# A hybrid decoder block in one pass: fp32r transposes, padded 64-row products, other first loads and separate loads in the output

## The chip, the cores and the metric

The kernel runs on one core of a Trainium2 chip. Its time is the device time of one execution in microseconds; where several executions are given, the median counts. The core has five engines that work side by side and wait for each other by semaphores: TensorE (PE) multiplies matrices out of SBUF into PSUM, VectorE (DVE), ScalarE (ACT) and GpSimd (POOL) work on rows, and SyncE (SP) issues the DMA transfers between device memory and SBUF.

## The reference

One block of a decoder, for one sequence of 1024 tokens with 1024 channels. The input is normalised and projected to 4104 columns. One half of the result feeds eight heads of stick-breaking attention, the other half four heads of a gated delta rule. Both results are normalised per head, gated, put side by side, projected back, added to the input and normalised.

```python
h = rmsnorm(x, norm1_w[layer])
proj = jnp.einsum('btd,de->bte', h, w_in[layer])
sb_q, sb_k, sb_v, sb_z, g_q, g_k, g_v, g_z, g_b, g_a = jnp.split(proj, split_idx, axis=-1)
...
o_sb = rmsnorm(o_sb.transpose(0, 2, 1, 3), sb_norm_w[layer]).reshape(b, t_len, SB_WIDTH)
o_sb = o_sb * jax.nn.silu(sb_z)
...
o_gdn = gated_delta_chunked(gq, gk, gv, decay, beta)
o_gdn = o_gdn * jax.nn.silu(g_z)
mixed = jnp.concatenate([o_sb, o_gdn], axis=-1)
x = x + jnp.einsum('bte,ed->btd', mixed, w_out[layer])
return rmsnorm(x, final_norm_w)
```

The attention weight of key s for query t is `sigmoid(z_ts)` times the product of `1 - sigmoid(z_tj)` over the keys between them. The delta rule works in chunks; for each chunk a unit lower triangular matrix is inverted, and a state of 128 by 128 per head runs from chunk to chunk.

## The kernel before

**Numbers.** Large products are made of three fp32r products: each operand is split into a high part (rounded to fp32r) and a low part (the rest), and high x high, high x low and low x high are summed in PSUM (`mm3`). The splitting is done by ACT (the rounding copy) and DVE or POOL (the subtraction). Small products are made in f32, which takes two passes each on TensorE.

**First stage.** x comes transposed in eight blocks of 128 channels (`xr`, from `xT`), beside the blocks of the query weights (`wq`) and the gain (`n1`). `LOADS` is the order in which the loads are issued, and `later` lets an operation in a queue only behind another one. Block 0 comes in two halves. Each block is scaled and split into `xh` and `xl`, and the eight query products grow in eight banks of PSUM. Meanwhile x comes a second time in rows, for the sums of squares. Then eight weight blocks `wcr` (columns of beta, decay and value) are split into the two halves of `chl`: the high part by ACT, the low part by DVE (blocks 0 and 1) or POOL (blocks 2 to 7), 520 columns at a time; the first 264 are used for the first value product, the others later, in `values`. When the norm is known, the raw blocks are scaled on DVE by gain and norm and split again into `xh` and `xl`.

**Fill.** The other projections are made in column groups of 128, in the order of the list `ORDER` (G: the delta heads' k, q and v; v: the second half of the values; k: attention keys; z: gates). They fill TensorE whenever no other stream has something ready.

**Delta rule.** For each head and half of the sequence, `gdn_pre` has q and k in a tile `kq` (four places in the pool `gd`), turns them on TensorE as f32 against the identity, and takes the sums of squares. `gdn_sub` and `gdn_inv` make the inverse of eight chunks: 16-row blocks by substitution on POOL, then 32, then 64, then 128 rows. The last step is two products per chunk over 64 rows: `y2p` from the lower left block of the matrix and the upper inverse (`W`, rows 0 to 63 of `wy`), and `x2p` from that and the lower inverse. The inverse stands in the tile `xinv` (`X`). `gdn_chain` then runs the state through the chunks.

**Attention.** For each head four windows of two query blocks; the scores are turned into weights by two sigmoids (ACT), a scan (DVE) and a product (POOL), then turned on TensorE as fp32r words (`turned`, with `Fixed.words`, which gives a second tile of type fp32r in the same place) and multiplied with the values.

**Output.** `out_weights` loads and splits the eight blocks of the output weights, first 4 to 7 (delta), then, once the projections are over, 0 to 3 (attention), in one stream. For each of the eight token blocks `enter_delta` loads the delta result (`mx`), the gate (`gt`) and the input row block (`xr`); `split` turns the four quarters of `mx` as f32 (`turned`), multiplies with the gate, and splits. `products_delta` adds 24 products per block to `xr`. `enter_attention`, `prepare(0)` and `products_attention` do the same for the attention half; the last adds the squares, multiplies by the inverse root and the final gain, and stores. `mx` and `gt` have three places in the pool `f0` and three in `f1`. The last block is cut in three pieces (512, 320 and 192 columns).

**Order.** The program writes the order of every engine by a planner of its own: the streams at the end of `block` are run by `interleave` against a model of the engines (`Model`, with a price for each operation in `cost`), and the order in which the model starts the operations is fixed for each engine. Streams with a smaller first number go first on TensorE; the second number is the priority of what they issue on the other engines. All DMA is issued on SP. So a change of a price or of a stream deals out the whole order anew. The profile puts almost every instruction on line 355, where the planner's recorder issues it; so the tiles' names tell them apart.

Of the kernel before, what the change touches and what calls it, by code (L numbers as in the profile page):

```python
# [28 lines left out]
ORDER = "G0 v1 G1 k0 k1 G2 G3 k2 k3 z4 z5 z6 z7 z0 z1 z2 z3".split()  # L29
# [104 lines left out]
class Fixed:  # L134
# [10 lines left out]
    def tile(self, shape, dtype, name, tag):  # L145
# [6 lines left out]
        return self.place(shape, dtype, name, at, r)  # L152

# [317 lines left out]
def block(tc, xT_d, x_d, n1_d, wE_d, wQ_d, wC_d, conv_d, alog_d, dtb_d, mixw_d, wo_d, fnw_d, out_d):  # L471
# [4 lines left out]
    with ExitStack() as top:  # L476
# [7 lines left out]
        fx = Fixed(ck, nc, {**{f"sg{w}": (2048 * (w + 1), 1) for w in range(4)}, "o2": (1024, 1)})  # L484
# [143 lines left out]
        for k in range(NK):  # L628
# [3 lines left out]
            xr = s0.tile([P, T], F32, name=f"xr{k}")  # L632
            raw.append(xr)
            n = 1 if k else 2
            for u in range(n):
# [6 lines left out]
                V.tensor_tensor(wl[:, es], w[:, es], wh[:, es].bitcast(F32), ALU.subtract)  # L642
                A.activation(xh[:, k, hs], xr[:, hs], AF.Copy, scale=n1[:, k:k + 1])
                V.scalar_tensor_tensor(xl[:, k, hs], xr[:, hs], n1[:, k:k + 1], xh[:, k, hs].bitcast(F32), ALU.mult, ALU.subtract)
# [21 lines left out]
        ck.prio = 0.4  # L666
        for b in range(NB):
# [39 lines left out]
        for k0 in range(0, NK, 2):  # L707
# [4 lines left out]
            for k in (k0, k0 + 1):  # L712
                A.activation(xh[:, k, :], raw[k], AF.Copy)
                V.tensor_tensor(xl[:, k, :], raw[k], xh[:, k, :].bitcast(F32), ALU.subtract)
# [229 lines left out]
        def delta_load():  # L944
            yield lambda: "dec" in flags
            for h in range(GH):
                for g in range(2):
# [6 lines left out]
                    kq = gd.tile([P, 4, 2, P], F32, tag="kq", bufs=4, name="kq")  # L954
# [33 lines left out]
        def gdn_pre(h, g):  # L988
# [10 lines left out]
            nkv = gd.tile([P, 4, P], F32, tag="nkv", bufs=4, name="nkv")  # L999
            for which in range(2):  # L1000
# [86 lines left out]
        def gdn_inv(h):  # L1087
# [30 lines left out]
            G.memset(W[0:32, :, 32:64], 0.0)  # L1118
            V.tensor_copy(W[0:32, :, 0:32], wc[0:32])
# [34 lines left out]
            for c in range(8):  # L1154
                TE.matmul(yv2[64:128, c, :], nm(c, slice(0, 64), slice(64, 128)), W[:, c, :], start=True, stop=True)
# [3 lines left out]
            for c in range(8):  # L1159
                TE.matmul(xv2[0:64, c, :], wy[64:128, c, :], X[64:128, c, 64:128], start=True, stop=True)  # L1160
# [203 lines left out]
        def out_weights():  # L1364
# [5 lines left out]
            yield lambda: "proj" in flags  # L1370
# [191 lines left out]
```

## Time and profile before

| | us |
|---|---|
| median of three executions | 658.06 |
| lowest and highest | 657.96, 659.88 |
| the profiled execution | 659.28 |
| its span, first to last instruction | 657.5 |

| engine | busy us | share | instructions |
|---|---|---|---|
| PE | 645.3 | 98% | 3978 |
| DVE | 453.8 | 69% | 851 |
| ACT | 387.5 | 59% | 921 |
| POOL | 332.2 | 51% | 364 |

The profile's page gives the engines' busy time, groups of instructions and DMA queues. In a row such as `pz<-step,mx 128*128 128x128 f32 x64 | 9.6, 272 | 0.0` stand the tile written and those read, for TensorE the held matrix (rows*columns) and the moving one, the count, the busy time in us, the mean duration of one in ns, and the idle time of the engine before them. All fp32r operands of products are printed as f32. Products overlap on TensorE, so a duration is longer than the distance to the next start. An f32 product or the like is recorded as two passes, a transpose as one. In a row of the timeline stand the start, the time from the first start to the last end, the engine, the instruction and how many of a kind follow each other. The granted clock is TensorE's, 1 for full speed.

### The profile page before, as it was taken

The numbers are of one execution on the slowest core, as the hardware profiler recorded it, in microseconds if no ns is written. First come the engines' busy times: TensorE is split into PE (matmuls) and PEld (weight loads), VectorE is DVE, ScalarE is ACT, GpSimd is POOL, SyncE is SP. The second block draws the span as 40 slices with busy tenths as digits, with TensorE's granted clock in tenths as the row PEclk, the third lists the DMA queues.
The fourth block names the chain that finished last, engine by engine and source line by source line (L and its number), as shares of the span: only waits on it lengthen the run. The fifth ranks groups of instructions, "written<-read, shape, count | busy, mean of one in ns | idle before, by whom it ended". The sixth has DMA issues, their size and how long they took to land.

```text
span 657.5 us, 11705 instructions
## 1 busy us (share of the span) xinstructions
PE 645.3 (98%) x3978; PEld 553.4 (84%) x3978; DVE 453.8 (69%) x851; ACT 387.5 (59%) x921; POOL 332.2 (51%) x364
## 2 busy tenths in 40 slices
PE   8999999999999999999999999999999999999995
PEld 7889888988888887888888888989898888888785
DVE  4358984434448879888889637897878553657874
ACT  5645566844538687777696447676878541223332
POOL 0106154928776857546586748473444323127642
PEclk9999999999999999999999999999999999999999
DMA  8929337863684435433563860634243492944232
GB/s 296 336 91 364 119 124 224 303 212 112 193 276 134 151 108 160 139 107 124 182 181 79 262 198 25 211 93 147 89 138 97 147 326 92 349 144 149 96 129 96
DMA packets 97643, 111.83 MB, mean 170 GB/s; under 512 B 29552, under 2 KB 62512, under 8 KB 97584
## 3 DMA queue, kind: packets, MB, share of 16 engines
q1 hardware_dynamic: 97584, 111.09, 51.7%
q8 instruction: 31, 0.51, 0.3%
q14 instruction: 28, 0.23, 0.1%
HBM read 76.03 MB, written 35.03 MB: 169 GB/s over the span
## 4 chain that ended last, share of the span: by engine, by line
PE 87%; DVE 8%; ACT 2%; issue 2%; DMA 1%; SPq 0%; POOL 0%; POOLq 0%; ACTq 0%; DVEq 0%
PE pp L355 53%; PE pz L355 25%; PE po L355 6%; PE pc L355 3%; DVE xl L355 2%; DVE xr L355 2%; DVE cc L355 1%; DMA xr<-xT 1%; DVE pp L355 1%; ACT yj L355 0%; DVE al L355 0%; SPq L355 0%; ACT nkv L355 0%; DVE v2e L355 0%; DVE ac L355 0%
## 5 line engine op out<-in xcount | busy, mean ns | idle before, releaser
L355 PE MATMUL pp<-xh,weh 128*128 128x512 f32 x360 | 148.8, 413 | 0.1
L355 PE MATMUL pp<-xl,weh 128*128 128x512 f32 x360 | 141.3, 392 | 0.5 <-DVE xl L355 0.3
L355 PE MATMUL pp<-xh,wel 128*128 128x512 f32 x360 | 141.3, 393 | 0.0
L355 POOL TENSOR_TENSOR sgf<-sgf,cc 128x128 f32<-128x128 f32 (+3 forms) x64 | 77.3, 1210 | 72.4 <-DVE cc L355 58.8
L355 POOL TENSOR_TENSOR wel<-wer,weh 128x512 fp32r<-128x512 f32 x48 | 62.1, 1298 | 57.0 <-ACT weh L355 49.8
L355 PEld LDWEIGHTS pp<-xh,wel 128*128 128x128 f32 x360 | 67.8, 188 | 14.9
L355 PEld LDWEIGHTS pp<-xl,weh 128*128 128x128 f32 x360 | 68.0, 189 | 10.9 <-DVE xl L355 1.3
L355 PEld LDWEIGHTS pp<-xh,weh 128*128 128x128 f32 x360 | 67.8, 188 | 10.4 <-DVE ac L355 0.8
L355 ACT ACTIVATE sgf<-pz,rs 128x384 f32<-128x384 f32 (+3 forms) x96 | 53.7, 589 | 13.2 <-PE pz L355 12.5
L355 DVE TENSOR_TENSOR_SCAN cc<-pz,step 128x384 f32<-128x384 f32 (+2 forms) x64 | 53.5, 846 | 9.2 <-ACT pz L355 8.9
L355 DVE TENSOR_TENSOR al<-pz,ah 128x512 fp32r<-128x512 f32 (+1 forms) x80 | 49.8, 628 | 12.8 <-ACT ah L355 12.6
L355 ACT ACTIVATE pz<-pz,ns 128x384 f32<-128x384 f32 (+3 forms) x96 | 52.8, 567 | 0.0
L355 PE MATMUL pp<-woh,mh 128*128 128x512 f32 (+2 forms) x132 | 52.2, 395 | 0.2 <-DVE xr L355 0.2
L355 ACT ACTIVATE ah<-pz 128x512 fp32r<-128x512 f32 (+1 forms) x80 | 43.7, 559 | 12.9 <-PE pz L355 12.7
L355 PE MATMUL pp<-woh,ml 128*128 128x512 f32 (+2 forms) x132 | 50.8, 385 | 0.0
L355 PE MATMUL pp<-wol,mh 128*128 128x512 f32 (+2 forms) x132 | 50.6, 383 | 0.0
L355 DVE SCALAR_TENSOR_TENSOR pp<-pre,conv,pp 128x512 f32<-128x512 f32 x42 | 31.5, 749 | 21.3 <-ACT pp L355 20.7
L355 POOL TENSOR_TENSOR ac<-ac,pre 128x512 f32<-128x512 f32 x24 | 31.0, 1291 | 29.3 <-ACT pre L355 20.1
L355 POOL TENSOR_TENSOR ml<-mf,mh 128x512 fp32r<-128x512 f32 x16 | 21.5, 1346 | 47.0 <-ACT mh L355 46.9
L355 PE MATMUL po<-ah,v2a 128*128 128x256 f32 (+1 forms) x160 | 43.5, 295 | 0.0
L355 DVE TENSOR_TENSOR_SCAN cc<-pz,cc,step 128x512 f32<-128x512 f32 (+1 forms) x32 | 38.7, 1208 | 3.6 <-ACT pz L355 3.0
L355 PE MATMUL po<-al,v2a 128*128 128x256 f32 (+1 forms) x160 | 39.4, 282 | 0.3 <-DVE al L355 0.3
(266 smaller groups left out, 1613.6 us busy)
## 6 DMA issues: line engine op xcount, KB each, us to landing
wer<-wE SPq DMA_DIRECT2D x48, 256.0 KB, 3.8
xr<-x SPq DMA_DIRECT2D x16, 512.0 KB, 7.2
g_s<-ac SPq DMA_DIRECT2D x24, 256.0 KB, 2.4
v_s<-v2e SPq DMA_DIRECT2D x16, 256.0 KB, 2.8
kq<-g_s SPq DMA_DIRECT2D x16, 256.0 KB, 3.9
v2a<-v_s SPq DMA_DIRECT2D x8, 512.0 KB, 4.5
q<-qk_s SPq DMA_DIRECT2D x8, 512.0 KB, 4.7
kh<-qk_s SPq DMA_DIRECT2D x8, 512.0 KB, 4.7
```

Of the source, the lines that this page charges most:

```text
L355: ins = f(*args, **kw).ins
```

## The change

- The four places of `kq` move from the pool `gd` to a fixed place in SBUF (`"kq": (4096, 4)`). The first four blocks of x stand there in the first stage, `kq` in the delta stage, and in the output stage a tile `mg` that holds a block's `mx` and `gt` together, for both halves of the output. `Fixed.room` tells whether a place is free.
- q and k, and the mix in `split`, are turned as fp32r words.
- The two 64-row products of the inverse run over 128 rows: the lower half of `wy` and the upper right block of `X` are set to zero on POOL (`X` for all heads but the first, as it starts as zero), and the operands are taken with all their rows.
- The gain's load is issued third instead of first, and for block 0 the low part of the weights goes ahead of that of x on DVE.
- The low parts of the weight blocks 2 to 7 are made on POOL in two pieces: 264 columns as before, 256 columns behind the second splitting of x block 4.
- In `ORDER`, `z4` goes ahead of `k2` and `k3`.
- The output weights of the attention half and the rows of x are loaded by streams of their own (`out_weights_attention`, `enter_x`), with other priorities and a separate tag.
- In `products_attention` a finished block is scaled by ACT into two banks of PSUM and multiplied with the gain by DVE in two halves, instead of in one DVE operation. For the last block, one sum of squares is added on POOL, EPS comes in with the last piece, and the second store is issued on ACT's DMA queue.

```diff
-ORDER = "G0 v1 G1 k0 k1 G2 G3 k2 k3 z4 z5 z6 z7 z0 z1 z2 z3".split()
+ORDER = "G0 v1 G1 k0 k1 G2 G3 z4 k2 k3 z5 z6 z7 z0 z1 z2 z3".split()
...
+    def room(self, tag):
+        return any(r is None or r.idle(self.ck.now) for _, r in self.slots[tag])
...
-            xr = s0.tile([P, T], F32, name=f"xr{k}")
+            xr = fx.tile([P, T], F32, f"xr{k}", "kq") if k < 4 else s0.tile([P, T], F32, name=f"xr{k}")
...
+                if k == 0:
+                    later(xlow, low)
...
-            (V if b < 2 else G).tensor_tensor(chl[b][:, 1, :], wc, chl[b][:, 0, :].bitcast(F32), ALU.subtract)
+            if b < 2:
+                V.tensor_tensor(chl[b][:, 1, :], wc, chl[b][:, 0, :].bitcast(F32), ALU.subtract)
+            else:
+                G.tensor_tensor(chl[b][:, 1, 0:264], wc[:, 0:264], chl[b][:, 0, 0:264].bitcast(F32), ALU.subtract)
+                wcs.append(wc)
...
+        first_loads[0:3] = first_loads[1:3] + first_loads[0:1]
...
+                if k == 4:
+                    for b, wc in enumerate(wcs, 2):
+                        later(G.tensor_tensor(chl[b][:, 1, 264:520], wc[:, 264:520], chl[b][:, 0, 264:520].bitcast(F32), ALU.subtract), again)
...
-                    TE.transpose(tp[:, j * P:(j + 1) * P], kq[:, j, which, :], ident)
+                    TE.transpose(tp[:, j * P:(j + 1) * P].bitcast(F32R), kw[:, j, which, :], idr)
...
+            G.memset(wy[64:128], 0.0)
...
+            if h:
+                G.memset(X[0:64, :, 64:128], 0.0)
...
-                TE.matmul(yv2[64:128, c, :], nm(c, slice(0, 64), slice(64, 128)), W[:, c, :], start=True, stop=True)
+                TE.matmul(yv2[64:128, c, :], nm(c, slice(0, P), slice(64, 128)), wy[:, c, :], start=True, stop=True)
...
-                TE.matmul(xv2[0:64, c, :], wy[64:128, c, :], X[64:128, c, 64:128], start=True, stop=True)
+                TE.matmul(xv2[0:64, c, :], wy[:, c, :], X[:, c, 64:128], start=True, stop=True)
...
-            yield lambda: "proj" in flags
+
+        def out_weights_attention():
+            yield lambda: "proj" in flags and "pool0" in flags
...
-            yield from weights_of(pools[1], range(4), "yr", 5)
+            yield from weights_of(pools[1], range(4), "wr", 2)
...
+        def block_inputs():
+            mg = fx.tile([P, 2, 512], F32, "mg", "kq")
+            return mg, mg[:, 0, :], mg[:, 1, :].rearrange("p (k t) -> p k t", k=4)
...
-            yield from turned(tp, [mx[:, j * P:(j + 1) * P] for j in range(4)])
+            mw = fx.words(mg, "mw")
+            yield from turned(tp, [mw[:, 0, j * P:(j + 1) * P] for j in range(4)])
...
+        def enter_x():
+            yield lambda: ("in", 0, 1) in ready
+            for b in range(NB):
+                yield lambda: b < 3 or "pool1" in flags
+                xs_[b] = block_tile(b, "xr")
+                S.dma_start(xs_[b], x_d[b * P:(b + 1) * P, :])
...
-                yield lambda: f"e{SBH - 1}{b // 2}" in flags and (b < 3 or (b - 3, 0) in ready)
+                yield lambda: f"e{SBH - 1}{b // 2}" in flags and ("in", NB - 1, 1) in ready and fx.room("kq")
...
-                    if n == 1:
-                        V.scalar_tensor_tensor(sy[:, 0:1], sy[:, 0:1], EPS, sy[:, 1:2], ALU.add, ALU.add)
+                    if n == 1 and last:
+                        G.tensor_tensor(sy[:, 0:1], sy[:, 0:1], sy[:, 1:2], ALU.add)
+                    elif n:
+                        V.scalar_tensor_tensor(sy[:, 0:1], sy[:, 0:1], EPS, sy[:, n:n + 1], ALU.add, ALU.add)
...
-                        S.dma_start(out_d[os_, 576:D], yf[:, 576:D])
+                        nc.scalar.dma_start(out_d[os_, 576:D], yf[:, 576:D])
...
-                        V.scalar_tensor_tensor(y, y, ry[:, 0:1], wts["fnw"], ALU.mult, ALU.mult)
+                        for u in range(2):
+                            us = slice(512 * u, 512 * u + 512)
+                            yb = (pc, po)[u]()
+                            A.activation(yb, y[:, us], AF.Copy, scale=ry[:, 0:1])
+                            V.tensor_tensor(y[:, us], yb, wts["fnw"][:, us], ALU.mult)
```

More of the change, by code (lines that the diff above doesn't have):

```diff
@@ L482, in open_pool @@
             return Pool(ck, ctx.enter_context(tc.tile_pool(name=name, bufs=1, **kw)), space, before)
-        fx = Fixed(ck, nc, {**{f"sg{w}": (2048 * (w + 1), 1) for w in range(4)}, "o2": (1024, 1)})
+        fx = Fixed(ck, nc, {**{f"sg{w}": (2048 * (w + 1), 1) for w in range(4)}, "o2": (1024, 1), "kq": (4096, 4)})
         cst = open_pool("cst")
@@ L999, in gdn_pre @@
             nkv = gd.tile([P, 4, P], F32, tag="nkv", bufs=4, name="nkv")
+            kw = fx.words(kq, "kw")
             for which in range(2):
```

48 lines of the change are left out of this document (23 added, 25 removed).

## The prediction

> **What bounds the kernel now.** I read the page's busy shares first, then the same by stretches, then what TensorE waited for.
>
> ```profile
> span 657.5 us, 11705 instructions
> PE 645.3 (98%) x3978; PEld 553.4 (84%) x3978; DVE 453.8 (69%) x851; ACT 387.5 (59%) x921; POOL 332.2 (51%) x364
> ```
> ```profile
> 0.00:12.00 12.00, 10.28 (x42) 8.30 (x42) 4.80 (x10) 5.82 (x8) 0.69 (x6) 1.00 0.72 251
> ...
> 50.00:84.00 34.00, 32.75 (x229) 30.25 (x228) 31.62 (x40) 17.96 (x30) 14.62 (x8) 1.00 0.64 232
> ...
> 204.00:255.00 51.00, 51.00 (x401) 44.41 (x400) 43.95 (x82) 38.06 (x89) 37.25 (x54) 1.00 0.41 127
> 255.00:266.00 11.00, 9.57 (x54) 8.02 (x53) 10.14 (x17) 8.44 (x21) 6.95 (x6) 0.84 0.72 219
> ...
> 520.00:650.00 130.00, 129.81 (x616) 107.21 (x615) 83.66 (x136) 41.24 (x75) 47.30 (x36) 1.00 0.51 174
> 650.00:657.50 7.50, 0.91 (x9) 0.74 (x7) 2.04 (x5) 1.80 (x7) 2.00 (x3) 0.80 0.29 114
> ```
> ```profile
> PE pz L355 <- DVE al L355: 1.0, 1, 1.0
> PE pp L355 <- POOL chl L355: 0.8, 1, 0.8
> ```
>
> The columns of the stretches are the length, then PE, weight loads, DVE, ACT and POOL busy, then granted clock and DMA. TensorE is the bound from 12 us to 650 us: in the stretches shown it stands still for 1.25 + 1.43 + 0.19 = 2.9 us. So a TensorE instruction that becomes shorter anywhere there is worth its saving in the span, as long as the other engines keep up. Three places are not of that kind: the first 12 us (loads), 50 to 84 us (DVE busy 31.62 of 34), and the last 7 us, where the products are over. And one patch is odd: in 255 to 266 us TensorE idles 11 - 9.57 = 1.43 us behind DVE, and the granted clock falls to 0.84, which costs another 0.16 x 11 = 1.76 us. Price of the patch: 3.2 us.
>
> Busy time of TensorE overstates one product, because products overlap. What one costs is the distance from its start to the next start. All costs below are such distances.
>
> **Transposes.** The 16 groups of four for the mix and the 16 for q and k, 64 transposes each, all become fp32r words. The f32 group of the mix, then a group that is fp32r already (the attention weights), both between 512-column products:
>
> ```profile
> L355 PE MATMUL pz<-step,mx 128*128 128x128 f32 x64 | 9.6, 272 | 0.0
> ...
> L355 PE MATMUL pz<-step,kq 128*128 128x128 f32 x64 | 8.6, 275 | 0.0
> ```
> ```profile
> 539.16 0.60 PE L355 MATMUL pz<-step,mx 128*128 128x128 f32 x4
> 539.52 0.47 PE L355 MATMUL pp<-xh,weh 128*128 128x512 f32 x1
> 539.83 0.39 PE L355 MATMUL pp<-xl,weh 128*128 128x512 f32 x1
> 540.06 0.39 PE L355 MATMUL pp<-xh,wel 128*128 128x512 f32 x1
> ```
> ```profile
> 402.24 0.46 PE L355 MATMUL pz<-step,stf 128*128 128x128 f32 x4
> 402.53 0.46 PE L355 MATMUL pp<-xh,weh 128*128 128x512 f32 x1
> 402.83 0.40 PE L355 MATMUL pp<-xl,weh 128*128 128x512 f32 x1
> ```
>
> A 512-column product takes 0.23 us (539.83 to 540.06). From the first transpose to the second product behind it are 0.67 us (f32) and 0.59 us (fp32r): the f32 group costs 0.67 - 0.23 = 0.44 us, the fp32r one 0.36, and by the unrounded starts 0.07 us lies between them. 32 groups x 0.07 = 2.3 us. The transposes sit where TensorE is the bound (the mix behind 520 us, q and k in the delta stage ahead of it), so I take all of it: -2.3, bounds -2.3 and 0 (none, if DVE takes over there). Copies behind a transpose read the same bank in the same shape; they cost nothing new.
>
> **The products of the inverse.** Two groups of 16 passes per head (8 f32 products, two passes each), four heads: 8 groups.
>
> ```profile
> 275.60 0.40 PE L355 MATMUL pp<-xh,wel 128*128 128x512 f32 x1
> 275.92 1.14 PE L355 MATMUL pz<-wy,dt 64*64 64x64 f32 x16
> 277.00 0.37 PE L355 MATMUL pz<-step,otf 128*128 128x128 f32 x2
> ```
> ```profile
> L355 PE MATMUL pz<-wy,dt 64*64 64x64 f32 x64 | 4.6, 221 | 0.0
> ```
> ```profile
> 100.45 0.39 PE L355 MATMUL pp<-xh,wel 128*128 128x512 f32 x1
> 100.68 0.27 PE L355 MATMUL pz<-step,cum 128*32 128x128 f32 x1
> 100.79 0.27 PE L355 MATMUL pz<-step,eg 128*32 128x128 f32 x1
> 100.82 0.48 PE L355 MATMUL pp<-xh,weh 128*128 128x512 f32 x1
> 101.14 0.39 PE L355 MATMUL pp<-xl,weh 128*128 128x512 f32 x1
> ```
>
> The product ahead of the 64-row group takes 0.32 us instead of 0.23, and 16 passes take 1.08 us; without the last one's 0.22 us the 15 distances are 0.92 us, 0.061 each with a slower first one, 0.058 by the unrounded starts, so 16 would be 0.93. Entering and leaving the shape therefore costs 0.09 + 0.15 = 0.24 us per group. What a 128-row pass with 64 columns on both sides takes is not in the trace. Below: 0.058 without the border, 8 x 0.24 = 1.9 us gained. Above: 0.11, the pace of a full f32 transpose (0.44 / 4), 16 x 0.11 = 1.76 against 1.08 + 0.09 = 1.17 us, or 8 x 0.59 = 4.7 us lost. I take the gain of 1.9, because the 128*32 rows have all rows and only 32 columns held: no pause ahead of it (0.23 us), and its two passes cost 101.14 - 100.68 - 0.23 = 0.23 us, 0.11 each with 128 columns moving; with 64 moving and 64 held, half of both, I expect half.
> The Trainium skill ("TensorEngine Tiling (Array Packing)", Key Properties) says that changing the tiling mode, not just the tile, drains TensorE, and it lists 128x64 and 128x32 as modes of their own; by that the padded groups keep their border and the gain of 1.9 is zero. The 128*32 rows above show no such pause, so the trace speaks against it for columns; no row has 64 columns with 128 rows.
>
> The zeros for the padding are seven POOL memsets of 64 x 512 (four of the one tile, three of the other): POOL is busy half of the span, and they are issued a stage ahead of the products that need them. I take nothing; if POOL is late, one group waits behind one long POOL operation of about 2 us (649.35 below shows two in 2.11), which other streams' products cover.
>
> **First loads.**
>
> ```profile
> 0.80 0.39 SPq L355 DMA_DIRECT2D n<-n  x1
> 1.25 0.42 SPq L355 DMA_DIRECT2D xr<-xT  x1
> ```
>
> The gain n goes third; the two loads that the first product needs are issued 0.45 us earlier. Everything up to 12 us hangs on loads, so I take -0.4, bounds -0.45 and 0. Splitting the first weights ahead of x helps only the first block of products; the second waits for its own load all the same: 0.
>
> **50 to 84 us.** The low parts of six weight blocks are made in halves on POOL, the second halves behind the fifth x block. The first halves remove the POOL wait of 0.8 us. But DVE is the bound here, and POOL and DVE hold each other up:
>
> ```profile
> 66.28 2.35 DVE L355 TENSOR_TENSOR xl<-xr,xh 128x1024 fp32r<-128x1024 f32 x1
> ...
> 69.75 1.21 DVE L355 TENSOR_TENSOR xl<-xr,xh 128x1024 fp32r<-128x1024 f32 x1
> ```
>
> The same operation takes 2.35 us beside POOL's work and 1.21 after it. What POOL no longer does early, it does later beside the last x blocks. Bounds: -1.25 (all of TensorE's idle time there) and +2.9 (half of the 1.14 us on each of five later operations). I take 0, as the POOL work is the same.
>
> **Order, loads and output stage.** One gate projection (48 products of 0.23, 11 us) moves ahead of two key projections; TensorE's work is the same, but attention of the later heads starts up to 11 us later.
>
> ```profile
> L355 PE MATMUL pz<-step,stf x288: 218/249/308, 204.9 to 520.1; 128*128 128x128 f32 x144
> ```
> ```profile
> L355 SPq DMA_DIRECT2D mx<-o_s x8: 319/320/687, 585.7 to 615.6; - x8
> ```
>
> Attention's last weights are turned at 520 us, its results are loaded from 585.7 us: 65 us of slack, so 0. The output blocks get four places shared with q and k instead of three and three of their own, and x and the second half of the output weights load apart from them, later in priority. TensorE has work for 129.81 of 130 us there; the scaling of a row by ACT and a product on DVE instead of one DVE operation lies beside it. 0; with that cover gone a late block costs its load, 5.7 us:
>
> ```profile
> gt<-gate_s SPq DMA_DIRECT2D x16, 256.0 KB, 5.7
> ```
>
> **The end.**
>
> ```profile
> 649.35 2.11 POOL L355 TENSOR_TENSOR yf<-xr,fnw 128x512 f32<-128x512 f32 x2 [2.00 <-DVE xr L355]
> ```
> ```profile
> 650.63 0.28 PE L355 MATMUL pp<-woh,ml 128*128 128x192 f32 x1
> 650.74 0.73 DVE L355 SCALAR_TENSOR_TENSOR sy<-sy 128x1 f32<-128x1 f32 x1 [0.81 <-ACT yj L355]
> 651.40 0.34 DVE L355 TENSOR_TENSOR xr<-pp,xr 128x192 f32<-128x192 f32 x1
> ...
> 653.89 0.81 SPq L355 DMA_DIRECT2D out<-yf  x2
> ```
>
> The last product ends at 650.91, but DVE adds it only at 651.40, because a one-column sum took 0.73 us until POOL let go (651.46). That sum goes to POOL, so the addition starts about 0.4 us sooner, and with it all that follows. The two last stores are issued one after the other in 0.81 us; the second goes to ACT's queue: 0.4 us. Together -0.8, bounds -0.9 and +0.4 (if ACT's queue is slower by as much).
>
> **The sum.** -2.3 - 1.9 - 0.4 + 0 + 0 - 0.8 = -5.4 us. The profiled execution took 659.28, so 653.9 beside it; it lay 1.2 above the median of the runs, 658.06, so the median goes to 652.7. The runs before spread from 657.96 to 659.88, 0.3%, or 2 us: less can't be told from no change.
>
> **Rivals.**
> - *The patch goes too.* The new order deals the DVE-heavy work out anew. For it: the stretches before and behind show no second one, so it hangs on a coincidence. Against: DVE is as busy as before (43.95 of 51 in 204 to 255). 652.7 - 3.2 = 649.5.
> - *Padding keeps its border* (the drain by columns): 652.7 + 1.9 = 654.6. Against it stand the 128*32 rows.
> - *Padded passes run at the full pace:* 652.7 + 1.9 + 4.7 = 659.3, within 0.3%.
> - *More patches.* TensorE's work shrinks by some 3 us in the delta stage, DVE's does not. Two more patches like that at 255 us: 652.7 + 6.4 = 659.1; three make it slower, 662.3. The Trainium skill ("TensorE: Matmul & The Clock Gate", Part 1) halves the clock only after about 3.4 us of idleness, by which a patch would cost its 1.4 us alone; here 1.43 us idle went with the clock at 0.84, and the row decides.
> - *The shared places run dry.* If two of the eight attention blocks are loaded late at 5.7 us each: 652.7 + 11.4 = 664.1, slower; one late block (5.7) already eats the gain. For it: six places become four. Against: a block is loaded long before its products.
>
> **How the numbers follow.** Forecast 0.44, patch gone 0.20, border kept 0.15, full pace 0.05, more patches 0.08 (of that 0.03 slower), places dry 0.08. Faster 0.44 + 0.20 + 0.15 = 0.79, within 0.3% 0.10, slower 0.11. The range goes from the patch gone with the 50 to 84 us bound (649.5 - 1.25, 648) to the border kept with one more patch (654.6 + 3.2, 657.5). The forecast by itself: 651 to 654.5.
>
> **What would show it.** Right: groups of four mix transposes at 0.36 us each between 512-column products; products of the inverse as 128 rows with no pause ahead and 0.93 us for 16 passes; ahead of the first product x issued at 0.8 us; the last addition directly behind the last product and two stores at the same time. Wrong: idle time of TensorE in 520 to 650 us behind the mix's loads, new stretches with a granted clock below 1, or padded passes at 0.11 us.

## The result, and the profile after

The changed kernel takes 661.98 us (median of six executions, 660.3 to 663.53), the kernel before 658.11 (six, 657.69 to 660.46). The ratio is 1.005, 95% interval 1.0026 to 1.0074: it became 0.5% slower where I forecast 0.8% faster. The profiled execution took 662.3 us.

First the page's busy shares of the changed kernel, then stretches that were shown of the kernel before (length, then PE, weight loads, DVE, ACT and POOL busy, granted clock, DMA), and one stretch more.

```profile
span 660.6 us, 11714 instructions
PE 643.6 (97%) x3978; PEld 551.9 (84%) x3978; DVE 449.2 (68%) x857; ACT 390.7 (59%) x933; POOL 339.8 (51%) x378
```
```profile
50.00:84.00 34.00, 29.46 (x210) 27.94 (x209) 29.67 (x38) 15.73 (x25) 19.42 (x14) 0.95 0.64 219
255.00:266.00 11.00, 10.61 (x72) 9.20 (x70) 10.76 (x21) 7.45 (x30) 11.00 (x9) 1.00 0.28 91
330.00:370.00 40.00, 38.34 (x221) 32.76 (x220) 31.47 (x61) 27.82 (x76) 28.89 (x37) 0.96 0.41 112
520.00:650.00 130.00, 129.50 (x650) 108.13 (x649) 86.63 (x150) 52.98 (x98) 47.73 (x36) 1.00 0.51 170
```

The same 40 us stretch of the kernel before, and TensorE's waits in two stretches of the changed one:

```profile
330.00:370.00 40.00, 39.47 (x247) 34.01 (x246) 33.23 (x59) 30.71 (x93) 30.37 (x44) 1.00 0.56 154
```
```profile
PE pp L358 <- DVE v2e L358: 2.7, 1, 2.7
PE pz L358 <- DVE xq L358: 1.8, 1, 1.8
```
```profile
PE pz L358 <- DVE cc L358: 0.9, 1, 0.9
PE pz L358 <- DVE oe L358: 0.7, 1, 0.7
```

The patch at 255 us is gone (10.61 busy, clock 1.00). Two others stand in its place. In 50 to 84 us TensorE now idles 4.54 us instead of 1.25, behind DVE, and then runs at half clock for 3.4 us (a clock of 0.95 over 34 us is 1.7 us lost, half of 3.4); in 330 to 370 us it idles 1.66 instead of 0.53, again with half clock behind it.

To see where the 3.6 us up to the last product go, I summed the distances between neighbouring starts on TensorE over each whole trace and split each distance into what the instruction needs, the idle time, the excess at half clock, and the rest (borders between shapes, 22.5 us in the changed kernel to 24.7 in e5). What the other instructions need is the same in all of them, 608.3 us, the first 5 us included.

| us up to the start of the last product | before | changed | e5 | e8 | e9 | e12 |
|---|---|---|---|---|---|---|
| transposes of q, k, mix | 13.95 | 11.26 | 11.26 | 11.26 | 11.26 | 11.26 |
| idle time | 3.98 | 9.25 | 4.82 | 8.17 | 4.02 | 6.04 |
| excess at half clock | 1.66 | 2.91 | 0.00 | 1.49 | 1.64 | 1.30 |
| all | 650.63 | 654.25 | 649.10 | 652.70 | 648.68 | 650.21 |

The transposes did become 2.69 us shorter. Idle time grew by 5.27 us and half clock by 1.25. So the question for the experiments was which part of the change makes TensorE wait. The milestones narrow it: the second group of 48 products of the fill (the second fill group below) starts 3.9 us later than before (91.85 against 87.97), the first product of the output 4.9 us later (561.07 against 556.19), the last product ends 3.6 us later (654.52 against 650.91).

### The profile page after: what moved, and what is told of

Its sections match the earlier page's. It is cut to its first block, busy times and chain, and to the rows that moved or that the text cites. A ratio compares the mean times of both kernels' runs of the same rounds, so it can differ in the third digit from the quotient of the medians.

```text
span 660.6 us, 11714 instructions
## 1 busy us (share of the span) xinstructions
PE 643.6 (97%) x3978; PEld 551.9 (84%) x3978; DVE 449.2 (68%) x857; ACT 390.7 (59%) x933; POOL 339.8 (51%) x378
## 4 chain that ended last, share of the span: by engine, by line
PE 69%; DVE 4%; issue 3%; ACT 3%; POOL 3%; DMA 1%; POOLq 0%; DVEq 0%; ACTq 0%
PE pp L358 46%; PE pz L358 16%; PE po L358 5%; PE pc L358 2%; DVE cc L358 1%; DMA wer<-wE 1%; POOL tt L358 1%; ACT sgf L358 1%; POOL sgf L358 1%; ACT pz L358 0%; DVE pp L358 0%; POOL ac L358 0%; DVE r2b L358 0%; POOL wel L358 0%; DVE xr L358 0%
## 5 line engine op out<-in xcount | busy, mean ns | idle before, releaser
L358 PE MATMUL pp<-xh,weh 128*128 128x512 f32 x360 | 150.4, 418 | 2.8 <-DVE v2e L358 2.7
L358 ACT ACTIVATE ah<-pz 128x512 fp32r<-128x512 f32 (+1 forms) x80 | 43.9, 561 | 24.3 <-PE pz L358 24.1
L358 PE MATMUL pp<-woh,mh 128*128 128x512 f32 (+2 forms) x132 | 51.5, 391 | 0.5 <-DVE xr L358 0.5
L358 ACT ACTIVATE weh<-wer 128x512 fp32r<-128x512 f32 x48 | 30.7, 640 | 20.2 <-PE pp L358 7.0
```

Source lines behind the costliest of these rows:

```text
L358: ins = f(*args, **kw).ins
```

## The experiments

The theory after the first comparison: the instructions are as cheap as I said, but the planner deals out a new order of all engines, and DVE's new order lets TensorE wait. Its rivals: an edit costs by itself (the halves, the memsets, the loads), or the delta stage gives shorter TensorE work back in any order.

### One at a time: transposes and padding in the old order, halves, loads, and all but the first stage

**e1_same_order.** The planner is told the old prices, so that only the instructions change:

```diff
-            return 58 if args[1].dtype == F32R else 108
+            return 58 if args[1].dtype == F32R and args[1].tensor.name[:2] not in ("kw", "mw") else 108
...
+            nc.gpsimd.memset(wy[64:128], 0.0)
```

> The kernel before with the transposes of q, k and the mix as fp32r words and the 64-row products padded to 128, and nothing else; the planner is told the old prices, so that TensorE, DVE, ACT and SP run the order of before. (The mix, one square and one product of the output move to the places of q and k.) Theory 1, the savings on TensorE are real and the changed kernel loses them by its new order and its first stage: 658.1 - 2.3 - 1.9 = 653.9 us, 0.994 of before. Theory 2, the savings do not become time because DVE and ACT hold the middle stage: 656.5 to 658 us, and the gaps of TensorE grow by what its instructions save.

Measured 659.65 against 659.76, ratio 1.0002 (0.9989 to 1.0015). Theory 1 (0.994) is out; the ratio lies where theory 2 ends, but the trace gives other reasons than theory 2 does. The padded groups show why half of the forecast is missing: they keep their border (shown at e7). And a memset is not free. Its rows on POOL, what DVE then waits for, and what TensorE waits for:

```profile
252.46 0.53 POOL L1120 MEMSET wy<- 64x512 f32 x1
253.07 1.55 POOL L355 TENSOR_TENSOR tt<-yx,xb 128x512 f32<-128x512 f32 x1
```
```profile
254.65 0.69 DVE L355 TENSOR_REDUCE xa<-tt 128x32 f32<-128x512 f32 x1 [0.89 <-POOL tt L355]
255.25 0.55 DVE L355 TENSOR_TENSOR al<-pz,ah 128x384 fp32r<-128x384 f32 x1
```
```profile
255.85 0.49 PE L355 MATMUL pz<-state,kqf 128*128 128x128 f32 x2 [0.54 <-DVE al L355]
```

The memset stands between two POOL operations of the substitution, DVE waits 0.89 us for the second, and TensorE 0.54 us for DVE. The profiled execution also began 1.55 us late behind its loads (first large product at 6.67 us instead of 5.12). So e1 leaves the gain of the transposes unclear; e5 repeats it without the padding.

**e2_halves_alone** and **e3_loads_alone** are the kernel before with one edit of the first stage each:

```diff
+                G.tensor_tensor(chl[b][:, 1, 0:264], wc[:, 0:264], chl[b][:, 0, 0:264].bitcast(F32), ALU.subtract)
...
+                        later(G.tensor_tensor(chl[b][:, 1, 264:520], wc[:, 264:520], chl[b][:, 0, 264:520].bitcast(F32), ALU.subtract), again)
```

> The kernel before with only the low weight parts made on POOL in two pieces. In the changed kernel TensorE waits 2.7 us at 79 us behind DVE (the value products' banks are read late) and then 3.4 us at half clock. Theory 1a, the later second pieces push DVE's scaling of x ahead of the reading of the banks: the wait of 2 to 3 us at 77 to 79 us and the half clock are here too, first filling group behind 78.5 us, 660.5 to 662.5 us in all unless the later order gives something back. Theory 1b, the first loads or the places of x do it: the first filling group starts at 75 to 76.5 us and there is no such wait.

```diff
+                    later(xlow, low)
...
+        first_loads[0:3] = first_loads[1:3] + first_loads[0:1]
```

> The kernel before with only the gain loaded third and the low part of the first weights ahead of that of x. In the changed kernel the norm's rows (rbc) landed at 54.3 us instead of 52.9, DVE waited for them, and the reading of the query banks behind it on DVE made TensorE wait 1.84 us at 56 us. Theory 1b, the first loads make rbc late: rbc lands behind 54 us and the wait at 56 us is here too, 659 to 660.5 us. Theory 1a: rbc lands by 53.3 us, no wait over 0.9 us at 55 to 59 us, 657.5 to 658.3 us.

The halves alone cost 1.06% (666.82 us, ratio 1.0106, 1.0084 to 1.0128), the loads nothing (659.12, ratio 0.9998, 0.9985 to 1.0011). The halves cost more than was expected: the second fill group comes 5.1 us later than before (93.03 against 87.97), the first output product 9.0 us later (565.23 against 556.19), so some 4 us are lost behind the first stage, in an order that is dealt anew there too; I did not take these apart. In the first stage TensorE waits as in the changed kernel:

```profile
PE pp L355 <- DVE v2e L355: 2.9, 1, 2.9
PE pz L355 <- DVE xq L355: 1.0, 1, 1.0
```

The POOL work is not the same, as I had assumed. POOL's low parts in the kernel before, first and last row, and then with the halves:

```profile
54.95 3.55 POOL L355 TENSOR_TENSOR chl<-wcr,chl 128x520 fp32r<-128x520 f32 x2 [28.06 <-DMA wcr<-wC]
...
65.23 2.32 POOL L355 TENSOR_TENSOR chlf<-wcr,chlf 128x520 fp32r<-128x520 f32 x1
```
```profile
55.38 0.75 POOL L355 TENSOR_TENSOR chl<-wcr,chl 128x264 fp32r<-128x264 f32 x1 [28.02 <-ACT chl L355]
...
72.61 1.72 POOL L355 TENSOR_TENSOR chlf<-wcr,chlf 128x256 fp32r<-128x256 f32 x1
```

Six operations of 520 columns took 12.7 us, twelve of half the size take 18.7 us (the sums over the rows of which the first and last are shown; from first start to last end 12.6 and 18.9): beside DVE's long operations a half takes 1.72 us where a whole one takes 2.3. But this alone does not make DVE late: one long DVE operation takes 1.75 us beside halves instead of 2.35. What else DVE does differently is its order. Rows of DVE before (first), with the halves (second):

```profile
52.88 1.29 DVE L355 SCALAR_TENSOR_TENSOR xr<-xr,n,rbc 128x1024 f32<-128x1024 f32 x1 [2.33 <-DMA rbc<-rs_s]
...
74.62 0.86 DVE L355 SCALAR_TENSOR_TENSOR v2e<-pp,rstd,v2e 128x256 fp32r<-128x256 f32 x2
```
```profile
70.28 5.14 DVE L355 SCALAR_TENSOR_TENSOR xr<-xr,n,rbc 128x1024 f32<-128x1024 f32 x3
...
78.55 0.86 DVE L355 SCALAR_TENSOR_TENSOR v2e<-pp,rstd,v2e 128x256 fp32r<-128x256 f32 x2
```

`v2e` reads the first two value banks, and the fill's first products need these banks. Before, six scalings and six low parts (`xr`, `xl`) stand ahead of it; with the halves all eight scalings and six low parts. Two more operations of 1.7 us each, and five more small sums (`smf`, 0.7 us together), are enough for the 3 us that TensorE waits. That is a second explanation beside the slower POOL, and e12 tests it.

**e4_first_stage_before.** The changed kernel with both edits of the first stage undone:

```diff
-        first_loads[0:3] = first_loads[1:3] + first_loads[0:1]
...
-                G.tensor_tensor(chl[b][:, 1, 0:264], wc[:, 0:264], chl[b][:, 0, 0:264].bitcast(F32), ALU.subtract)
+            (V if b < 2 else G).tensor_tensor(chl[b][:, 1, :], wc, chl[b][:, 0, :].bitcast(F32), ALU.subtract)
```

> The changed kernel with the first stage of before (gain first, low parts of x and the first weights as before, low weight parts on POOL in one piece); x blocks 0 to 3 keep their new places. Theory 1: the first filling group starts at 76 to 76.5 us again, 3 us earlier, and no half clock at 80 us: 662.0 - 3.9 = 658.1 us or less. Theory 2: no faster than 660.5 us, as the time is lost behind 84 us.

661.89 us, ratio 1.0034 (1.0022 to 1.0047): not clearly faster than the changed kernel, as theory 2 had it. The second fill group starts at 88.65 us, 3.2 us earlier than in the changed kernel. But the last product starts only 0.4 us earlier (653.83 against 654.25): a new place has taken the gain. TensorE's largest wait in 340 to 380 us:

```profile
PE pz L358 <- ACT o2f L358: 2.5, 1, 2.5
```

Another 0.7 us for DVE follow, and half clock for two windows of 3.4 us.

So the first stage is one place where time is lost, and the middle, dealt anew again, is another.

### The transposes with the order held, and dealt anew

**e5_transposes_and_end** has the fp32r words of e1 and the end, and nothing else:

```diff
-                    TE.transpose(tp[:, j * P:(j + 1) * P], kq[:, j, which, :], ident)
+                    TE.transpose(tp[:, j * P:(j + 1) * P].bitcast(F32R), kw[:, j, which, :], idr)
...
+                    if n == 1 and last:
+                        G.tensor_tensor(sy[:, 0:1], sy[:, 0:1], sy[:, 1:2], ALU.add)
...
-                        S.dma_start(out_d[os_, 576:D], yf[:, 576:D])
+                        nc.scalar.dma_start(out_d[os_, 576:D], yf[:, 576:D])
```

> The kernel before with the fp32r transposes (q, k and the mix) and the edits of the last row (one-column sum on POOL, second store in ACT's queue); no padding, no other first loads, no halved low parts, and the order of every engine as before. Theory A: the transposes are worth what their rows say where no new wait is dealt in: the groups of eight cost 0.705 us instead of 0.878 and those of four 0.365 instead of 0.440, 2.7 us in all, of which the run with the same order showed some 0.5 us by 187 us and 0.6 to 1.0 us in the output stage; the end is worth 0.6. So 1.7 to 3.0 us faster than before, ratio 0.995 to 0.9975, with the patch at 261 us still there. Rival B: TensorE's shorter instructions are given back in any order, because DVE and POOL set the pace of the delta stage; then only the mix and the end stay, 1.2 us, ratio 0.998 or more, and the milestone of the first output product is where it was before.

657.37 us against 659.77, ratio 0.9965 (0.9944 to 0.9985): 2.3 us faster. That is theory A. Rival B is not: the first output product starts 1.1 us sooner than before (555.08 against 556.19), although this execution fell some 1.0 us behind that of e9, which has the same order there, between 199 and 213 us, beginning with a wait for a load.

**e8_transposes_dealt_anew** is e5 without the first diff line of e1, so the planner knows the new price:

> The same instructions as the run with the transposes and the end, but the planner is told the shorter price of the new transposes and deals the order of all engines anew from the delta stage on. Theory A: the gain of the transposes is the same, and what the new dealing does to the waits decides: idle time of TensorE and stretches at half clock differ from the held order by -2 to +6 us, and the time follows them, so 655 to 663 us. Rival B: the order matters little (the dealing before was no better than any other); then the time is within 0.5 us of the held order, and idle time plus half clock too.

660.77 us in the same series, ratio 1.002 (1.0003 to 1.0037): 3.4 us slower than e5 with the same work on every engine. Idle time is 8.17 us instead of 4.82, half clock 1.49 instead of 0. The largest new wait:

```profile
353.50 1.10 PE L355 MATMUL pz<-kqf 128*128 128x256 f32 x4 [2.70 <-DVE dt L355]
```

This shows that the order alone, with the same instructions, eats more than the transposes bring.

**e6_two_waits_less** moves three DVE instructions of e5 by hand:

```diff
+            ops.insert(n, ops.pop(ops.index(scaled[0])))
+        ops.insert(318, ops.pop(319))
+        ops.insert(320, ops.pop(321))
```

> The run with the transposes and the end, and three DVE instructions put elsewhere in DVE's own order: the scaling of the first x block by the broadcast row scale goes behind the last three copies of q out of the banks, and at 260 us the low part of the attention weights and the state update each go ahead of one convolution product. Theory A: a wait is made by what is queued ahead on DVE, so the 0.96 and 0.44 us at 261 and 262 us lose some 0.45 us together, and if that is enough to spare the half clock (3.4 us at 0.5), 1.7 us more; nothing at 56 us, where before has no such wait. So 0.4 to 2.2 us below the run without the three moves, ratio 0.992 to 0.997 to before. Rival B: the patch follows from all the work DVE has there (10.14 of 11 us), and three moved instructions only move the wait: within 0.3 us of the run without them.

658.39 us, ratio 0.9977 (0.9959 to 0.9996): no better than e5, as far as the overlapping intervals tell. Neither this execution nor that of e5 had half clock there, so what sparing it would bring was not tested. The largest wait in 255 to 266 us:

```profile
PE pp L355 <- DVE ac L355: 0.7, 1, 0.7
```

The wait for `al` fell from 1.0 to 0.6 us, and this one, for the convolution product that now stands later, came in. That is rival B's mechanism: where DVE has work for the whole stretch, moving it moves the wait. The time lies 1.0 us above e5's, outside rival B's 0.3 us, but within the spread of the executions.

### What the border belongs to

**e7_128_columns_held** is the kernel before with the padding, and the first product of each pair widened:

```diff
-                TE.matmul(yv2[64:128, c, :], nm(c, slice(0, 64), slice(64, 128)), W[:, c, :], start=True, stop=True)
+                TE.matmul(yv2[:, c, :], nm(c, slice(0, P), slice(0, P)), wy[:, c, :], start=True, stop=True)
```

> The kernel before with the padding alone, the order of every engine but POOL's memsets as before, and the first product of each padded pair widened from 64 to all 128 columns held (its upper 64 result rows are left unused); the second one holds 64 columns as the change has it. Theory A: the pause at the border belongs to the 64 columns held and not to the 64 rows, so the widened four groups have the product ahead at 0.23 us and no slow first and last pass, while the other four keep 0.32 ahead and 1.07 us for 16 passes. A widened pass takes between 0.058 us (64 columns moving) and 0.11 (the pace of a full f32 transpose): four groups cost between 0.24 us less and 0.6 us more each, so the kernel is between 1.0 us faster and 2.4 us slower than before, plus up to 0.7 us of waits behind the memsets. Rival B: the pause comes from the small f32 product itself (64 columns moving); then the widened groups keep 0.32 us ahead and a first pass of 0.1 us as well.

One group of each kind, on TensorE:

```profile
277.18 0.39 PE L356 MATMUL pp<-xh,wel 128*128 128x512 f32 x1
277.41 1.89 PE L356 MATMUL pz<-wy,dt 128*128 128x64 f32 x16
279.11 0.34 PE L356 MATMUL pz<-step,otf 128*128 128x128 f32 x2
...
281.12 0.40 PE L356 MATMUL pp<-xh,wel 128*128 128x512 f32 x1
281.45 1.15 PE L356 MATMUL pz<-xinv,wy 128*64 128x64 f32 x16
282.52 0.38 PE L356 MATMUL po<-ah,v2a 128*128 128x256 f32 x1
```

With 128 columns held the product ahead takes 0.23 us and the first pass is no slower than the others: no border. With 64 held the product ahead takes 0.33 and the 16 passes 1.07 us, as with 64 rows. But a wide pass takes 0.11 us, so 16 take 1.70: the widened group costs 0.53 us more than the one with a border (1.70 + 0.23 against 1.07 + 0.33). Theory A holds. The kernel was slower than its upper bound of 2.4 + 0.7 us: 664.67, ratio 1.0065 (1.0041 to 1.0088), 4.3 us; in its profile 2.1 us are the four groups, 0.5 a wait of the kind shown for e1, and for the rest I found no single place.

### The output stage, the moved projection

**e9_output_stage_too** is the changed kernel without the padding, the first stage's edits and the moved projection, the planner told the old price. **e10_gate_ahead_too** adds the moved projection. **e11_changed_gate_behind** is the changed kernel with only that undone. The edit of the order, in e9 and e11, and the first of the others in e9:

```diff
-ORDER = "G0 v1 G1 k0 k1 G2 G3 z4 k2 k3 z5 z6 z7 z0 z1 z2 z3".split()
+ORDER = "G0 v1 G1 k0 k1 G2 G3 k2 k3 z4 z5 z6 z7 z0 z1 z2 z3".split()
...
-            G.memset(wy[64:128], 0.0)
...
+            return 58 if args[1].dtype == F32R and args[1].tensor.name[:2] not in ("kw", "mw") else 108
```

> The changed kernel without three of its parts (no padding, first loads and low parts as before, the gate projection behind the key projections as before) and with the planner told the old price of a transpose, so that the order of every engine is that of the kernel before up to the output stage; there it has the change's four shared places, separate loads and the scaling in halves, and the change's end. Theory A: the output stage's own edits are worth something, as the changed kernel took 93.45 us from its first output product to its last and the run with the transposes and the end 94.29: 0.3 to 1.0 us below that run, so a ratio to before of 0.995 to 0.9965. Rival B: the changed kernel's output stage was short only because it started later, with its loads long there; then the ratio is that of the run with the transposes and the end, 0.9965, or above. Rival C, of the prediction: shared places run dry, idle time of TensorE behind loads of the mix in 540 to 650 us; then 1 us or more is lost against the run without.

657.37 us, ratio 0.9966 (0.995 to 0.9982), the same as e5. From the first output product to the last it took 93.0 us, e5 94.3: in the profiles the output stage gained 1.3 us. The medians do not show it, but the interval of the ratio holds all that theory A forecast (0.995 to 0.9965) and rival B as well, and half clock at 262 us, which came in this execution and not in e5's, takes 1.6 us. So what the output stage's edits are worth stays open. No wait behind a load of the mix stands in 540 to 650 us, which rules out rival C.

> The run before this one with one more part of the change: the gate projection z4 ahead of the key projections k2 and k3. Theory A: what is dealt between 284 and 540 us changes by it, and such a new dealing is what turned the changed kernel's gain into waits (0.90 and 0.70 us at 355 us with half clock behind them): 1 to 4 us slower than the run without it, ratio to before 0.997 to 1.002. Rival B: the place of the projection is free, as its 48 products are the same; then within 0.5 us of the run without it, and no new wait above 0.5 us.

659.1 us in the same series, ratio 0.9994 (0.9981 to 1.0007), 1.7 us slower than e9, by two intervals that just touch: theory A. The profiled execution began 1.4 us later behind its loads, which is not the edit's doing; in 385 to 535 us idle time is 1.51 us instead of 0.25. The wait that makes most of it is one for POOL, which e9 does not have:

```profile
PE pp L358 <- POOL wel L358: 1.0, 1, 1.0
```

> The changed kernel with one part undone: the gate projection z4 behind the key projections again. Theory A (two causes, the halved low parts in the first stage and any new dealing of the middle, each enough to eat the gain): undoing this one part leaves the waits at 56 and 79 us as they are, and the middle is dealt anew once more; ratio to before 1.002 to 1.008, as the changed kernel's 1.005. Rival B: the moved projection is the cause of what was lost in the middle; then the first output product comes 2 us or more sooner than in the changed kernel (561.07 us), and the ratio is 1.002 or less.

663.27 us, ratio 1.006 (1.0035 to 1.0085): undoing the moved projection alone brings nothing, the first output product comes at 561.27 us as in the changed kernel (561.07). It gave one more thing. In this execution the broadcast row scale arrived at 52.4 us, 1.9 us earlier than in the changed kernel's, and the value banks were still read late. DVE's rows, and TensorE's wait:

```profile
52.44 1.28 DVE L358 SCALAR_TENSOR_TENSOR xr0f<-xr0f,n,rbc 128x1024 f32<-128x1024 f32 x1 [2.07 <-DMA rbc<-rs_s]
...
69.55 5.13 DVE L358 SCALAR_TENSOR_TENSOR xr<-xr,n,rbc 128x1024 f32<-128x1024 f32 x3
...
77.81 0.86 DVE L358 SCALAR_TENSOR_TENSOR v2e<-pp,rstd,v2e 128x256 fp32r<-128x256 f32 x2
```
```profile
PE pp L358 <- DVE v2e L358: 3.4, 1, 3.4
```

So a late row scale is not what causes the wait at 79 us. The wait at 56 us is another matter: it is gone here, and it was 1.8 us in the changed kernel's execution, where the row scale arrived at 54.3 us.

### Five DVE instructions

**e12_banks_read_sooner** is the whole changed kernel with the last two scalings put behind the reading of the two banks (five of the small sums come behind it too), in DVE's order only:

```diff
+        moved = [low, read[0], read[1], scaled[6], scaled[7]]
+        for o in moved:
+            ops.remove(o)
+        n = ops.index(gas[1]) + 1
+        ops[n:n] = moved
```

> The changed kernel, all of it, with five DVE instructions in another order by hand: the last two of the eight scalings of x go behind the reading of the first two value banks (the small sums stay ahead of it), so that 12 long operations stand ahead of that reading as in the kernel before, and not 14. Every other engine keeps its order. Theory A: the wait at 79 us comes from these two scalings, not from the halved low parts; the first bank is read at 75.3 to 76.5 us instead of 78.63, TensorE's wait of 2.70 us falls below 0.6 with no half clock behind it, and the second fill group starts at 88 to 89.5 us instead of 91.85. If that is kept to the end, the kernel is 2.5 to 4 us faster than the changed one, ratio to before 0.998 to 1.001. Rival B: the halves on POOL (18.7 us of POOL instead of 12.7) hold DVE up whatever its order; then the bank is read at 77 us or later and the wait stays above 1.5 us, ratio 1.003 to 1.006. Rival C: the wait goes, and what is gained is lost again in the middle; then the second fill group is 2.5 us or more sooner, but the last product within 1.5 us of the changed kernel's 654.52.

657.85 us against 659.05, ratio 0.998 (0.9966 to 0.9993). The changed kernel had 1.005; the two intervals lie apart. The stretch, DVE's first scaling and first reading of a bank in the changed kernel, and the same two rows here:

```profile
50.00:84.00 34.00, 34.00 (x239) 32.16 (x238) 32.02 (x43) 18.88 (x31) 20.83 (x15) 1.00 0.66 236
```
```profile
54.33 1.28 DVE L358 SCALAR_TENSOR_TENSOR xr0f<-xr0f,n,rbc 128x1024 f32<-128x1024 f32 x1 [4.27 <-DMA rbc<-rs_s]
...
78.63 0.86 DVE L358 SCALAR_TENSOR_TENSOR v2e<-pp,rstd,v2e 128x256 fp32r<-128x256 f32 x2
```
```profile
51.56 1.28 DVE L358 SCALAR_TENSOR_TENSOR xr0f<-xr0f,n,rbc 128x1024 f32<-128x1024 f32 x1 [0.95 <-DMA rbc<-rs_s]
...
72.58 0.87 DVE L358 SCALAR_TENSOR_TENSOR v2e<-pp,rstd,v2e 128x256 fp32r<-128x256 f32 x2
```

TensorE is busy for all 34 us, with POOL's halves in it as long as ever (20.83 us of POOL). The second fill group starts at 85.74 us, 6.1 us sooner. Of this 2.8 us are luck, since the row scale came that much earlier here than in the changed kernel's execution. Counted from the first scaling the luck drops out: the bank is read 21.7 us behind it before, 24.3 in the changed kernel (25.4 in e11) and 21.0 here. So 3.3 us are the order's, with the halves in place: theory A, and rival B is out. The last product ends 4.0 us sooner than in the changed kernel (650.48 against 654.52). That is less than the 6.1 us, as 2 us more were lost on the way, but far more than rival C allows. The patch at 351 us is untouched (0.9 and 0.7 us, then half clock).

## Why the prediction was wrong

**50 to 84 us: "I take 0, as the POOL work is the same."** This is the step that failed most. The POOL work was not the same (18.7 us instead of 12.7), and that did not matter. What mattered is that the edit made the planner put two more scalings ahead of the reading of the banks: a wait of 2.7 us, and half clock behind it (some 1.6 us, the 2.91 of the table less the 1.30 that e12 keeps), together above my upper bound of 2.9. e2 shows that the edit alone brings this wait, e12 that DVE's order is the reason. The other wait in this stretch, 1.8 us at 56 us, goes with the row scale, whose landing varies between executions: it is gone in e11 and e12, which have the same loads, where the row scale landed sooner. One part held: POOL's wait of 0.8 us is gone.

**Order: "TensorE's work is the same ... so 0."** I had written in the text ahead of the prediction that a change of a price or of a stream deals the whole order anew, and then priced the edits as if it stood. The same edit, transposes and end, is worth 2.3 us in the old order (e5) and costs 1.3 in a new one (e8). The moved projection costs 1.7 us where it is added to e9 (e10), and undoing it in the changed kernel brings nothing (e11). These figures do not add up to the changed kernel's 3.3 us, as each edit deals a new order; how much of the loss belongs to which edit in the changed kernel itself stays open.

**Transposes, -2.3 us.** The size was right: a mix group of four between 512-column products takes 0.29 + 0.30 - 0.23 us in the changed kernel,

```profile
566.52 0.46 PE L358 MATMUL pz<-step,mwf 128*128 128x128 f32 x4
566.81 0.46 PE L358 MATMUL pp<-woh,mh 128*128 128x512 f32 x1
567.11 0.40 PE L358 MATMUL pp<-wol,mh 128*128 128x512 f32 x1
```

0.36 us as forecast, 2.69 us in all. What failed is "so I take all of it": that held only as long as nothing else moved. There e5 gave 2.3 us (1.0 to 3.7) for the transposes and the end, whose rows sum to 3.3.

**Padding, -1.9 us.** It gained 0, as in the rival "padding keeps its border". A padded group in the changed kernel:

```profile
388.77 0.39 PE L358 MATMUL pp<-xh,wel 128*128 128x512 f32 x1
389.09 1.15 PE L358 MATMUL pz<-xinv,wy 128*64 128x64 f32 x16
```

The product ahead still takes 0.32 us. My evidence against the border, the 128*32 rows, were two transposes of one pass each, not two passes of one product; they are no model for 64 held columns. By the Trainium skill ("TensorEngine Tiling (Array Packing)", Key Properties) a change of the tiling mode drains TensorE; e7 agrees: 128x64 has the border, 128x128 has none. Why the 32-column transposes show no border, no run here tells; as a witness for a product of another shape they were too weak to speak against the border.

**First loads, -0.4 us.** x is issued at 0.8 us as forecast, but the first large product starts at 5.08 us instead of 5.12, and e3 measures nothing. **The end, -0.8 us.** From the last product to the end of the span 6.06 us instead of 6.63: -0.57. The last addition and the two stores are where I put them:

```profile
654.56 0.36 DVE L358 TENSOR_TENSOR xr<-pp,xr 128x192 f32<-128x192 f32 x1 [0.79 <-PE pp L358]
...
656.93 0.33 SPq L358 DMA_DIRECT2D out<-yf  x1
657.08 0.38 ACTq L1540 DMA_DIRECT2D out<-yf  x1
```

**The rivals.** "More patches" came true in kind: waits at 56, 79 and 355 us. That its price for three, 662.3, lies beside the median of 661.98 is luck: idle time and half clock grew by 6.5 us and not by 9.6, and the padding's missing 1.9 us and the smaller gains of the loads and the end make up most of the rest. It had a chance of 0.08; the stretches before showed one patch, but they showed it in one dealing of the order, and say nothing on the next. The upper end of my range was added up wrongly as well (654.6 + 3.2 is 657.8, not 657.5); the result lies above either. "The patch goes too" came true as well, and was outweighed. "The shared places run dry" did not happen: TensorE is busy for 129.50 of the 130 us behind 520 us.

**The account.** In the two profiles the transposes give -2.69 us, waits and half clock +6.52, borders -0.2 and the end -0.57: together +3.0 us, from a span of 657.5 to one of 660.6.

## What to carry to other kernels

Where a planner deals the order, price an edit in two parts: what its instructions save, and what a new dealing may cost; for the transposes in this kernel the second was 3.4 us (e8 against e5), more than the first. Measure an edit with the order held before judging it, and then look at what stands ahead of the reading that frees a bank: five instructions put elsewhere by hand turned 0.5% slower into 0.2% faster. When a row is taken as a witness for a new operation, it must have the same kind and held shape; a transpose does not stand for a product.

## What the runs showed of the hardware

- An f32 product with 64 held columns on 128 rows has the same border as one of 64 rows (0.32 us for the product ahead, 1.07 us for 16 passes); with 128 held and 64 moving columns there is none, and a pass takes 0.11 us instead of 0.058.
- DVE and POOL slow each other on long operations: beside POOL's whole low parts a DVE operation of 1.27 us takes 2.35, beside the halves 1.75. The Trainium skill ("SBUF — State Buffer", Terms) says that the port shared by the two is locked for a whole instruction. Full exclusion would give about 1.27 + 1.78 = 3.05 and 1.27 + 0.75 = 2.02 us with POOL's own 1.78 and 0.75 us; the rows show less, so the two do overlap in part.
- The same two waits, 0.96 and 0.44 us at 261 us, were followed by half clock in some executions and not in others. The stretch 255 to 266 us of e5, and of e9:

```profile
255.00:266.00 11.00, 9.57 (x60) 7.74 (x60) 10.78 (x19) 8.74 (x21) 7.19 (x7) 1.00 0.69 206
```
```profile
255.00:266.00 11.00, 9.56 (x52) 7.88 (x51) 10.34 (x17) 8.56 (x21) 6.58 (x6) 0.84 0.78 226
```

The excess is some 1.6 us. The Trainium skill ("TensorE: Matmul & The Clock Gate", Part 1) has a free-running window of 3413 ns, and the half clock lasts 3.41 us here; but it asks for a window of idleness, and 1.4 us of idle time were enough in e9.
- The landing of the broadcast row scale varied between 51.5 and 54.4 us over the fourteen traces, and the wait at 56 us went with it where the first stage was the same: 1.8 us at 54.3 (changed kernel), none at 52.4 (e11) and 51.5 (e12).
